# Ten low parts of weights formed by adding DMAs, and the first conv-out chunk split: a hybrid decoder layer on one core

## The chip, the cores and the metric

The kernel runs on 1 core of a Trainium2 chip. The metric is the device time of one execution in microseconds; the time before is the median of three runs.

## The reference, cut to what matters

One layer over 256 tokens of width 1024, float32 throughout. `n` is an RMS norm of the input. A combined projection of `n` gives a convolution branch, an attention branch and two gates; then come a cross attention, an MLP and a last norm.

```python
u = a * sigmoid(gate)                                    # conv branch, from n @ w_in
u = depthwise_conv(u, conv_w, 31 taps, causal) + conv_b
u = silu(layernorm(u, ln_g, ln_b))
y_conv = u @ w_conv_out
y_attn = top_k_attention(q, k, v, qi, ki, wi) @ w_attn_out   # 8 heads
h = x + (g_conv * y_conv + g_attn * y_attn) @ w_mix_out
h = h + cross_attention(rmsnorm(h), rmsnorm(mem))        # 4 heads, wx_q, wx_kv, wx_o
h = h + square(relu(rmsnorm(h) @ w_ff1)) @ w_ff2
return rmsnorm(h)
```

## The kernel before, in words

**Weights.** All weights come as a stream of chunks of 1 MB (128 partitions x 2048 float32), in the order of `STREAM` (line 34): conv 0 to 3, qi, ki, conv 4 to 7, gc (the gate of the conv branch), ga (the gate of the attention branch), v, q and k in turn, xk and xv (cross attention's keys and values), ao (attention out), co (conv out), mix, xq, xo, f1 and f2. Numbered from 0, chunk 8 is conv 5, chunk 35 is ao 0 and chunk 39 is co 0. `load` (line 154) issues a chunk's DMA on the SP queue into one of three `raw` buffers; chunks named in `EARLY` (line 58) get a buffer of their own out of a larger pool.

**Splitting.** A product in float32 is made of three products in float32r. Each chunk is split in two halves of 128x1024: ScalarE copies the half rounded to the high part `hi` (line 178), VectorE subtracts it from the raw half to give the low part `lo` (line 181). `high` does the first and queues the second as a job; `split_ahead` (line 213), called once in every tile, takes one low job and then one high job, so that up to five halves are ready ahead of TensorE. Six buffers of each part rotate. With the last low part of a chunk, the chunk's raw buffer is done with, and `load` is called for the next chunk. A tile of weights then is 8 steps of the contraction with three products each: high x high, high x low, low x high (`mm3`, line 247).

**Two whole chunks.** Chunks in `WHOLE` (line 59), conv 0 and co 0, are not split; their products run in float32 with the activations as they are (`form_b_whole`, line 302, for co 0). Its 16 products stand as 32 records in the trace.

**Forms.** `form_b` (line 274) does a chunk in two tiles of 24 products, each into one bank of PSUM out of `ps_mm`, which has two banks (tag "mm", line 141); after a tile its bank is evicted by ScalarE or VectorE (`after`). `form_b_late` (line 285) does both tiles but for the last steps of the contraction, then the last steps of both, then both evictions. `form_b_whole` took its two banks from `ps_acc`, which has four. `form_a` (line 569) does v and xv in quarters.

**Chains and fillers.** `tick` (line 218), called after each tile, lets every running chain (a generator: an attention head, the layer norm, the memory's norm) go one step on, and then fills VectorE with convolution taps out of `fill`, as long as the priced VectorE work stands behind the priced TensorE work (`Counted`, line 62). One tap is one `scalar_tensor_tensor` of VectorE; when a channel tile has its 31 taps, POOL adds it to `usum` (line 455). With the last of the eight tiles the chain `layer_norm` (line 595) is started: TensorE averages over channels (`ps_mub`), VectorE subtracts, ScalarE squares, TensorE sums (`ps_vr`), POOL takes the power (`rs_vr`), and, once all eight heads are done, ScalarE loads the Silu table, TensorE spreads the factors (`ps_rsb`), VectorE multiplies and ScalarE applies eight Silu (lines 620 to 625). Then `parts_of` (line 631) splits the result `u_p` in four steps of VectorE, one at a tick. co 0 as a whole chunk needs only the Silu's result, `acc`; co 1 to 3 need `u_p`.

**Around the change.** After the heads come four ao chunks (eight tiles, evicted by ScalarE to `ya`, line 318), then co; each co tile is gated by VectorE (`gated`, line 717) and split for mix.

Of the kernel before, what the change touches and what calls it, by code (L numbers as in the profile page):

```python
# [8 lines left out]
F32 = mybir.dt.float32  # L9
F32R = mybir.dt.float32r  # L10
BF16 = mybir.dt.bfloat16
AF = mybir.ActivationFunctionType
ALU = mybir.AluOpType
# [5 lines left out]
S = 256  # L19
KT = D // P  # L20
# [13 lines left out]
STREAM = (  # L34
    [("conv", i) for i in range(4)]
    + [("qi", i) for i in range(2)]
    + [("ki", 0)]
    + [("conv", i) for i in range(4, 8)]
    + [("gc", i) for i in range(4)]
    + [("ga", i) for i in range(4)]  # L40
    + [("v", i) for i in range(4)]
    + [(n, i) for i in range(4) for n in ("q", "k")]
# [12 lines left out]
NK = 72  # L55
N_CHUNK = KT * S
HALVES = 6
EARLY = (3, STREAM.index(("co", 0)))
WHOLE = (("conv", 0), ("co", 0))


class Counted:
# [49 lines left out]
def block_kernel(ctx, tc, x, xt, mem, memt, wst, wki, vecs, convw, gout, out):  # L112
    nc = tc.nc
    ctx.enter_context(tc.manual_schedule())
    pe = Counted(nc.tensor, pe_price)
    dve = Counted(nc.vector, dve_price)
    act = nc.scalar.activation
# [10 lines left out]
    def t8(name, dt=F32, shape=(P, KT, S)):  # L128
        return big.tile(list(shape), dt, tag="t8", bufs=12, name=name)
# [7 lines left out]
    def bank(tag, bufs, name):  # L137
        return psum.tile([P, 512], F32, tag=tag, bufs=bufs, name=name)
# [4 lines left out]
    def ps_acc(name):  # L143
        return bank("acc", 4, name)
# [5 lines left out]
    prepared, whole = {}, {}  # L150
# [3 lines left out]
    def load(parts=1):  # L154
        if nload[0] >= len(STREAM):
            return
        c = nload[0]
        nload[0] += 1
        key = STREAM[c]
        raw = t8(f"raw{c}", F32, (P, N_CHUNK)) if c in EARLY else raws.tile([P, N_CHUNK], F32, tag="raw", name=f"raw{c}")  # L160
        n = KT * NK if key[0] == "ki" else N_CHUNK
        src = wki if key[0] == "ki" else wst[INDEX[key]]
        for q in range(parts):
            ns = slice(q * n // parts, (q + 1) * n // parts)
            nc.sync.dma_start(raw[:, ns], src[:, ns])
        if key in WHOLE:
            whole[key] = raw.rearrange("p (k n) -> p k n", k=2 * KT)
            return
        parts = 1 if key[0] == "ki" else 2
        for q in range(parts):  # L170
            ns = slice(q * n // parts, (q + 1) * n // parts)
            high_jobs.append(lambda ns=ns, q=q, last=q == parts - 1: high(key, c, raw, ns, q, last))

    def high(key, c, raw, ns, q, last):
        n = ns.stop - ns.start
        hi = highs.tile([P, N_CHUNK // 2], F32R, tag="hi", name=f"hi{c}_{q}")[:, :n]
        lo = lows.tile([P, N_CHUNK // 2], F32R, tag="lo", name=f"lo{c}_{q}")[:, :n]
        act(hi, raw[:, ns], AF.Copy)  # L178

        def low():  # L180
            dve.tensor_tensor(out=lo, in0=raw[:, ns], in1=hi.bitcast(F32), op=ALU.subtract)
            prepared[(*key, q)] = (hi, lo)
            if last and c not in EARLY:
                load()

        low_jobs.append(low)

    def split_high():
        if high_jobs and nsplit[0] - nused[0] < HALVES - held[0]:
            nsplit[0] += 1  # L190
            high_jobs.pop(0)()

    def split_low():
        if low_jobs:
            low_jobs.pop(0)()
# [17 lines left out]
    def split_ahead():  # L213
        if not waiting[0]:
            split_low()
        split_high()

    def tick():
        for c in list(chains):
            if next(c, "end") == "end":  # L220
                chains.remove(c)
        while (len(fill) > 1 or (fill and (len(done) > 5 or nused[0] < 5))) and dve.total < pe.total - 1000:
            fill_one()
        dve.total = max(dve.total, pe.total - 2000)
# [10 lines left out]
    def finish(chain):  # L235
        while chain in chains:
            tick()

    def start(gen):
        chains.append(gen)  # L240
        return gen
# [28 lines left out]
    def is_wide(kind, ct):  # L270

        return kind == "f1" or (kind == "mix" and ct < 6)

    def form_b(kind, i, x2, after, ps_of=ps_mm):

        for ct in range(2):
            w = weights(kind, i, ct, KT)
            split_ahead()
            ps = ps_of(f"ps_{kind}{i}{ct}")
            wide = is_wide(kind, 2 * i + ct)  # L280
            tile_b(ps, w, x2, wide=wide)
            after(2 * i + ct, ps if wide else ps[:, :S])
            tick()

    def form_b_late(kind, i, x2, after, cuts=(KT - 1,), ps_of=None):
# [12 lines left out]
            after(2 * i + ct, banks[ct] if is_wide(kind, 2 * i + ct) else banks[ct][:, :S])  # L298
            tick()
        held[0] = 1  # L300

    def form_b_whole(kind, i, x, after, cuts):

        w = whole[(kind, i)]
        banks = [ps_acc(f"ps_{kind}{i}{ct}")[:, :S] for ct in range(2)]
        for lo, hi in zip((0, *cuts), (*cuts, KT)):
            for ct in range(2):
                for kt in range(lo, hi):
                    pe.matmul(banks[ct], w[:, ct * KT + kt, :], x[:, kt, :], start=kt == 0, stop=kt == KT - 1)
            split_ahead()  # L310
            if hi == KT:
                load()
            tick()
        for ct in range(2):
            after(2 * i + ct, banks[ct])

    def copy_to(dst):
        return lambda ct, ps: act(dst[:, ct, :], ps, AF.Copy)
# [120 lines left out]
    acc = t8("acc")  # L439
    usum = cst.tile([P, S], F32, tag="sums", bufs=2, name="usum")  # L440

    def tap(t, s):
        def go():
            j = TAPS - 1 - s
            if s == 0:
                act(acc[:, t, :], u[:, t, :], AF.Identity, scale=cw[:, t, j : j + 1], bias=cvb[:, t : t + 1])
            else:
                dve.scalar_tensor_tensor(out=acc[:, t, s:], in0=u[:, t, : S - s], scalar=cw[:, t, j : j + 1],
                                         in1=acc[:, t, s:], op0=ALU.mult, op1=ALU.add)
            if s == TAPS - 1:  # L450
                done.append(t)
                if len(done) == KT:
                    start(layer_norm())
                if len(done) > 1:
                    nc.gpsimd.tensor_tensor(out=usum, in0=usum if len(done) > 2 else acc[:, done[0], :],
                                            in1=acc[:, t, :], op=ALU.add)
        return go

    def conv_tile(i, half):
        key = ("conv", i)  # L460
        w = weights("conv", i, half, KT) if key not in WHOLE else None
        split_ahead()
# [8 lines left out]
    def conv_in(i):  # L471
# [8 lines left out]
        fill.append([tap(i, s) for s in range(1, TAPS)])  # L480
        if ("conv", i) in WHOLE:
            load()
# [105 lines left out]
        form_a("v", hf, n2, v_rm, (1.0, 1.0))  # L588


    u2 = []

    normed = []

    def layer_norm():
        u2.append(parts_t8("u_p"))
        yield
        mub = ps_aux("ps_mub")[:, :S]
        pe.matmul(mub, onesd, usum, start=True, stop=True)
        mub = mub.unsqueeze(1).to_broadcast([P, 2, S])  # L600
        vs = w2("vs", F32, (P, 2, S))
        pairs = [slice(2 * c, 2 * c + 2) for c in range(4)]
        for c, cs in enumerate(pairs):
            dve.tensor_tensor(out=acc[:, cs, :], in0=acc[:, cs, :], in1=mub, op=ALU.subtract)
            sq = vs if c == 0 else w2(f"sq_vr{c}", F32, (P, 2, S))
            act(sq, acc[:, cs, :], AF.Square)
            if c > 1:
                dve.tensor_tensor(out=vs, in0=vs, in1=before, op=ALU.add)
            before = sq
        waiting[0] = True  # L610
        yield
        waiting[0] = False
        dve.tensor_tensor(out=vs, in0=vs, in1=before, op=ALU.add)
        dve.tensor_tensor(out=vs[:, 0, :], in0=vs[:, 0, :], in1=vs[:, 1, :], op=ALU.add)
        yield
        rs = rsqrt(vs[:, 0, :], "vr")
        yield
        while len(headed) < NH:
            yield
        act(table, table, AF.Silu)  # L620
        rsb = spread(rs, "rsb").unsqueeze(1).to_broadcast([P, 2, S])
        for c, cs in enumerate(pairs):
            dve.tensor_tensor(out=acc[:, cs, :], in0=acc[:, cs, :], in1=rsb, op=ALU.mult)
            for t in (2 * c, 2 * c + 1):
                act(acc[:, t, :], acc[:, t, :], AF.Silu, scale=lng[:, t : t + 1], bias=lnb[:, t : t + 1])
        normed.append(True)
        for c in range(4):
            yield
            parts_of(2 * c)
# [52 lines left out]
    for i in range(4):  # L682
        q, k = qk(f"q{i}"), qk(f"k{i}")
# [20 lines left out]
        form_b("ao", i, o2, copy_to(ya))  # L704
    while fill:
        fill_one()
    while not normed:
        tick()


    h_t = t8("h_t")
# [18 lines left out]

    gate_branch(0)
    for i in range(4):
        if i == 0:
            form_b_whole("co", i, acc, gated, (2, 4, 6))
        else:
            form_b("co", i, u2[0], gated)
    low_due.pop()()


# [277 lines left out]
    for c in range(14):  # L1017
# [4 lines left out]
        for k in range(2):  # L1022
            w = weights("f2", c, k, 1)
# [102 lines left out]
```

## Time and profile before

| | before |
|---|---|
| median of 3 runs | 516.89 us (516.72 to 516.94) |
| the profiled execution | 516.86 us |
| its span | 515.1 us |
| granted TensorE clock, mean | 0.998 |
| busy: TensorE matmul / weight load | 504.3 / 463.1 us |
| busy: VectorE / ScalarE / POOL | 419.4 / 286.9 / 19.2 us |
| moved by DMA | 92.75 MB |

Lines of the profile read so: the engine, the operation, what it writes and reads by the program's names, shapes, then a count, busy time and mean. In a chain or timeline the first number is the start within the span and the second how long it took, both in us. In the list of waits the numbers behind the colon are us in total, times, longest. PE is TensorE, PEld its weight loads, DVE VectorE, ACT ScalarE, POOL GpSimd, SP SyncE; a small q behind it is the engine's queue. L77 is a helper that records most VectorE and TensorE operations, so groups are told apart by their tiles.

### The profile page before, as it was taken

What the parts mean: (1) busy time and instruction counts of PE and PEld (TensorE: products, weight loads), DVE (VectorE), ACT (ScalarE), POOL (GpSimd) and SP (SyncE); (2) the same over time, 40 slices, a digit from 0 to 9 for tenths busy, and PEclk for the clock granted to TensorE, in tenths of its full rate; (3) what the DMA queues carried; (4) which work ended last, traced back from release to release, by engine and by line L of the source; (5) the groups of instructions that cost most, each with busy time, mean ns of one, the idle gap of its engine ahead of it and who ended that gap; (6) DMA issues with size and microseconds to landing.
All of it is one profiled execution on the core that took longest, in us unless ns stands there. A gap on an engine that the chain in (4) does not pass through costs nothing.

```text
span 515.1 us, 8515 instructions
## 1 busy us (share of the span) xinstructions
PE 504.3 (98%) x3354; PEld 463.1 (90%) x3354; DVE 419.4 (81%) x796; ACT 286.9 (56%) x489; POOL 19.2 (4%) x30
## 2 busy tenths in 40 slices
PE   7999999999999999999999999999999999999995
PEld 5999999999899999999999998988888888888884
DVE  4998999999988999999898976696766566666565
ACT  5666655546446666656655657565654454554442
POOL 2000000001001000021000000000000000000000
PEclk9999999999999999999999999999999999999999
DMA  8856435464552343454744541446445554445402
GB/s 317 359 187 236 155 122 205 174 225 183 194 216 102 144 164 118 155 224 161 275 143 155 207 184 44 181 165 242 164 169 220 221 207 163 164 174 219 181 1 81
DMA packets 14311, 92.75 MB, mean 180 GB/s; under 512 B 1584, under 2 KB 2480, under 8 KB 3776
## 3 DMA queue, kind: packets, MB, share of 16 engines
q1 hardware_dynamic: 13952, 91.85, 48.3%
q8 instruction: 26, 0.43, 0.3%
q10 hardware_dynamic: 288, 0.33, 0.2%
q14 instruction: 13, 0.11, 0.1%
q0 software_dynamic: 32, 0.04, 0.0%
HBM read 91.16 MB, written 1.05 MB: 179 GB/s over the span
## 4 chain that ended last, share of the span: by engine, by line
PE 95%; issue 1%; ACT 1%; DVE 1%; DMA 1%; POOL 0%; POOLq 0%; DVEq 0%; ACTq 0%
PE ps_f L77 17%; PE ps_ff L77 16%; PE ps_conv L77 9%; PE ps_co L77 5%; PE ps_ao L77 4%; PE ps_ga L77 4%; PE ps_gc L77 4%; PE ps_k L77 4%; PE ps_q L77 4%; PE ps_mix L77 4%; PE ps_v L77 4%; PE ps_xo L77 3%; PE ps_xq L77 2%; PE ps_qi L77 2%; PE ps_xk L77 2%; PE ps_xv L77 2%
## 5 line engine op out<-in xcount | busy, mean ns | idle before, releaser
L77 DVE TENSOR_TENSOR lo<-raw,hi 128x1024 fp32r<-128x1024 f32 x161 | 195.7, 1225 | 3.3 <-ACT hi L178 1.6
L178 ACT ACTIVATE hi<-raw 128x1024 fp32r<-128x1024 f32 x161 | 166.4, 1047 | 2.5 <-PE ps_v L77 2.5
L77 DVE SCALAR_TENSOR_TENSOR acc<-u,cw,acc 128x255 f32<-128x255 f32 (+27 forms) x240 | 100.6, 475 | 0.6
L77 PE MATMUL ps_f<-ff_p,hi 128*128 128x512 f32 x256 | 89.8, 396 | 0.0
L77 PE MATMUL ps_ff<-hi,fs 128*128 128x512 f32 (+1 forms) x256 | 80.8, 387 | 0.0
L77 PE MATMUL ps_f<-ff_p,lo 128*128 128x256 f32 x256 | 66.2, 279 | 0.0
L77 PEld LDWEIGHTS ps_ff<-hi,fs 128*128 128x128 f32 x256 | 47.9, 188 | 9.2
L77 PEld LDWEIGHTS ps_f<-ff_p,hi 128*128 128x128 f32 x256 | 46.8, 188 | 9.2
L77 DVE TENSOR_TENSOR ft<-ps_f,ft 128x256 f32<-128x256 f32 x32 | 13.6, 423 | 46.4 <-ACT ft L957 46.4
L77 PEld LDWEIGHTS ps_f<-ff_p,lo 128*128 128x128 f32 x256 | 48.2, 188 | 2.6
L957 ACT ACTIVATE ft<-ps_f 128x256 f32<-128x256 f32 x32 | 12.2, 380 | 66.9 <-PE ps_f L77 66.9
L77 PE MATMUL ps_ff<-lo,fs 128*128 128x512 f32 (+1 forms) x128 | 49.4, 386 | 0.0
L77 PE MATMUL ps_conv<-n_p,hi 128*128 128x256 f32 x224 | 41.0, 285 | 0.0
L77 PEld LDWEIGHTS ps_conv<-n_p,hi 128*128 128x128 f32 x224 | 34.9, 192 | 0.8 <-issue 0.7
L77 PE MATMUL ps_conv<-n_p,lo 128*128 128x256 f32 x112 | 31.7, 283 | 0.0
L77 PEld LDWEIGHTS ps_ff<-lo,fs 128*128 128x128 f32 x128 | 24.1, 188 | 4.9
L77 PE MATMUL ps_q<-n_p,hi 128*128 128x256 f32 x128 | 24.4, 291 | 0.0
L77 PE MATMUL ps_ao<-o_p,hi 128*128 128x256 f32 x128 | 23.5, 285 | 0.0
L77 PE MATMUL ps_k<-n_p,hi 128*128 128x256 f32 x128 | 23.4, 284 | 0.0
L77 PE MATMUL ps_gc<-n_p,hi 128*128 128x256 f32 x128 | 23.1, 283 | 0.0
L77 PE MATMUL ps_ga<-n_p,hi 128*128 128x256 f32 x128 | 23.1, 283 | 0.0
L77 PE MATMUL ps_mix<-mix_p,hi 128*128 128x512 f32 (+1 forms) x80 | 22.1, 350 | 0.0
(229 smaller groups left out, 1003.3 us busy)
## 6 DMA issues: line engine op xcount, KB each, us to landing
raw<-in_wst_dram SPq DMA_DIRECT2D x80, 1024.0 KB, 4.8
raw<-in_wst_dram SPq DMA_DIRECT2D x4, 512.0 KB, 7.7
x_rm<-in_x_dram SPq DMA_DIRECT2D x2, 512.0 KB, 3.9
mem_rm<-in_mem_dram SPq DMA_DIRECT2D x1, 1024.0 KB, 9.0
mem_t<-in_memt_dram SPq DMA_DIRECT2D x1, 1024.0 KB, 11.0
h_t<-in_xt_dram SPq DMA_DIRECT2D x1, 1024.0 KB, 6.9
out_dram<-hg SPq DMA_DIRECT2D x4, 176.0 KB, 2.2
g_out<-in_gout_dram SPq DMA_DIRECT2D x1, 512.0 KB, 7.0
```

What stands on the lines that cost most here:

```text
L77: return fn(*args, **kwargs)
L178: act(hi, raw[:, ns], AF.Copy)
L957: act(t, ps[:, S:], AF.Copy)
```

## The change: ten DMAs that add, and one chunk split

For the second half of chunks 8, 11, 14, and so on to 35, ScalarE writes the negated high part into the low part's buffer right behind the high part, and the low job issues a DMA on POOL's queue that adds the raw half to it. The other low parts stay on VectorE. co 0 is no longer whole: it is split as every chunk is, read through one of the three raw buffers, and done in `form_b_late` (its cut is before the last of the eight steps) with the split activations. `form_b_whole` goes away. Ahead of co the program waits for the whole layer norm chain, parts and all, where it waited only for the Silu.

```diff
-EARLY = (3, STREAM.index(("co", 0)))
-WHOLE = (("conv", 0), ("co", 0))
+EARLY = (3,)
+WHOLE = (("conv", 0),)
...
+    def low_by_dma(key, c, q):
+
+        return q == 1 and c % 3 == 2 and 8 <= c < STREAM.index(("ao", 1))
+
     def high(key, c, raw, ns, q, last):
...
         act(hi, raw[:, ns], AF.Copy)
+        by_dma = low_by_dma(key, c, q)
+        if by_dma:
+            act(lo, hi.bitcast(F32), AF.Copy, scale=-1.0)
 
         def low():
-            dve.tensor_tensor(out=lo, in0=raw[:, ns], in1=hi.bitcast(F32), op=ALU.subtract)
+            if by_dma:
+                nc.gpsimd.dma_start(lo.bitcast(F32), raw[:, ns], accum_op=ALU.add)
+            else:
+                dve.tensor_tensor(out=lo, in0=raw[:, ns], in1=hi.bitcast(F32), op=ALU.subtract)
             prepared[(*key, q)] = (hi, lo)
             if last and c not in EARLY:
                 load()
...
-    def form_b_whole(kind, i, x, after, cuts):
...
                 if len(done) == KT:
-                    start(layer_norm())
+                    norms.append(start(layer_norm()))
...
-    while not normed:
-        tick()
+    finish(norms[0])
...
     for i in range(4):
-        if i == 0:
-            form_b_whole("co", i, acc, gated, (2, 4, 6))
-        else:
-            form_b("co", i, u2[0], gated)
+        (form_b_late if i == 0 else form_b)("co", i, u2[0], gated)
```

The low job priced itself to `Counted` as VectorE work; the DMA does not, so the fillers take that room and the taps, and with them the layer norm, come earlier in the built order.

More of the change, by code (lines that the diff above doesn't have):

```diff
@@ L300, in form_b_late @@
         held[0] = 1
-    def form_b_whole(kind, i, x, after, cuts):
[L304 to L312, printed above, removed]
-            tick()
-        for ct in range(2):
-            after(2 * i + ct, banks[ct])
     def copy_to(dst):
@@ L588, in block_kernel @@
         form_a("v", hf, n2, v_rm, (1.0, 1.0))
-    u2 = []
-    normed = []
+    u2, norms = [], []
     def layer_norm():
@@ L625, in layer_norm @@
                 act(acc[:, t, :], acc[:, t, :], AF.Silu, scale=lng[:, t : t + 1], bias=lnb[:, t : t + 1])
-        normed.append(True)
         for c in range(4):
@@ L706, in block_kernel @@
         fill_one()
-    while not normed:
-        tick()
+    finish(norms[0])
     h_t = t8("h_t")
```

## The prediction

> **What bounds the kernel now.** I read the page first: the span, the busy sums and the shares of the chain that ended last. The profiled execution took 516.86 us around its span of 515.1 us; the median shown is 516.89, so the two are one number here, and the sum below is made against 516.86.
>
> ```profile
> span 515.1 us, 8515 instructions
> ...
> PE 504.3 (98%) x3354; PEld 463.1 (90%) x3354; DVE 419.4 (81%) x796; ACT 286.9 (56%) x489; POOL 19.2 (4%) x30
> ...
> PE 95%; issue 1%; ACT 1%; DVE 1%; DMA 1%; POOL 0%; POOLq 0%; DVEq 0%; ACTq 0%
> ...
> L77 DVE TENSOR_TENSOR lo<-raw,hi 128x1024 fp32r<-128x1024 f32 x161 | 195.7, 1225 | 3.3 <-ACT hi L178 1.6
> L178 ACT ACTIVATE hi<-raw 128x1024 fp32r<-128x1024 f32 x161 | 166.4, 1047 | 2.5 <-PE ps_v L77 2.5
> ```
>
> The reader is to see that TensorE makes 95% of the chain. VectorE's 161 subtractions, which the change thins out, cost 1.225 us each but stand on no link of it. The second view is the list of waits of TensorE itself:
>
> ```profile
> PE ps_warm L350 <- DVE zero_r L335: 1.9, 1, 1.9
> PE pt_n L77 <- DVE ms_n L77: 1.3, 1, 1.3
> PE ps_xo L77 <- ACT xptr L853: 0.8, 1, 0.8
> PE pt_n L77 <- DVE x_rm L77: 0.4, 1, 0.4
> ```
>
> Three of these are the start, the third is in the cross attention near 314 us. So in the first half TensorE never waits for VectorE: **12 us less VectorE work is worth nothing by itself**. It can only pay through the products that TensorE is then given. The chain in order of time shows those:
>
> ```profile
> 75.73 23.04 PE ps_gc L77 x192
> ...
> 121.81 21.79 PE ps_v L77 x96
> ...
> 219.13 0.67 PE ps_o L77 x6
> 219.80 5.49 PE ps_xv L77 x24
> 225.29 11.51 PE ps_ao L77 x96
> 236.81 0.43 PE ps_mub L77 x2
> ...
> 242.99 0.34 PE ps_vr L77 x4
> ...
> 246.30 0.22 PE ps_rsb L77 x2
> 246.52 2.87 PE ps_ao L77 x24
> 249.39 24.18 PE ps_co L77 x176
> ```
>
> **The change part by part.** *The first conv-out chunk.* A tile of split weights is 24 products; 192 of them take 23.04 us, so 0.120 us each and 2.88 us a tile. The conv-out stage holds 176 records in 24.18 us: 144 split products (six tiles, 17.28 us) and 32 records of the whole float32 chunk, which leaves 6.90 us. Split, that chunk is 48 products, 5.76 us. **Gain 1.14 us.** It adds two halves on ScalarE (2 x 1.05 us) and two on VectorE (2 x 1.225 us), both hidden behind attention-out products as the other chunks' halves are.
>
> *The layer norm moves.* In the built order of the changed program the product of the mean (ps_mub) no longer stands after four attention-out tiles but right after the last head (ps_o), ahead of the last two quarters of xv; ps_vr follows them, then one attention-out tile, then ps_rsb, then the other seven. So the parts of u are done many tiles before conv-out needs them, which answers the question whether splitting makes conv-out wait. But the norm's work on ScalarE moves too, and that part was last seen here:
>
> ```profile
> 246.34 0.38 ACT L318 ACTIVATE ya<-ps_ao 128x256 f32<-128x256 f32 x1 [1.74 <-PE ps_ao L77]
> 246.73 1.28 ACT L620 ACT_TABLE_LOAD   x1
> 248.02 0.20 ACT L620 ACTIVATE table<-table 128x1 f32<-128x1 f32 x1
> 248.13 4.03 ACT L625 ACTIVATE acc<-acc,vec 128x256 f32<-128x256 f32 x8
> 252.07 1.04 ACT L178 ACTIVATE hi<-raw 128x1024 fp32r<-128x1024 f32 x1
> 253.02 0.36 ACT L318 ACTIVATE ya<-ps_ao 128x256 f32<-128x256 f32 x1
> ```
>
> From ps_rsb at 246.30 until the next eviction is over at 253.38 ScalarE needs 7.08 us: table load, eight Silu, a high part, the eviction. Before, this was the last attention-out tile; conv-out went on into other PSUM banks (ps_acc, four) and nobody waited. After, six more attention-out tiles follow, and their pool (ps_mm) has two banks. Counted from ps_rsb: 0.22 for it, 2.87 for the second tile, 2.88 for the third, so the fourth tile could start at 5.97 but needs the bank of the second, which is free at 7.08 plus some 0.04 for the signal. **Loss 1.15 us**, a new wait. Queued behind the Silu on ScalarE are the high part and that eviction; behind TensorE's wait stands the whole rest of its stream. After it, the third tile's eviction comes a high part later (1.0 + 0.4 us) while the fourth tile takes 2.88, so it does not repeat.
>
> *The variance.* ps_vr must wait until the squares are summed. Before, the norm's VectorE chain ran from 237.28 to 242.41:
>
> ```profile
> 237.28 1.88 DVE L77 TENSOR_TENSOR acc<-acc,ps_mub 128x512 f32<-128x512 f32 x3 [0.23 <-PE ps_mub L77]
> ...
> 241.99 0.42 DVE L77 TENSOR_TENSOR vs<-vs 128x256 f32<-128x256 f32 x1
> ...
> 258.09 0.42 DVE L77 TENSOR_TENSOR gc_t<-ps_co,gc_t 128x256 f32<-128x256 f32 x1
> ```
>
> ```profile
> 219.84 0.38 ACT L244 ACTIVATE o_p<-ps_o 128x256 fp32r<-128x256 f32 x1 [1.97 <-PE ps_o L77]
> ...
> 231.09 0.38 ACT L318 ACTIVATE ya<-ps_ao 128x256 f32<-128x256 f32 x1 [1.55 <-PE ps_ao L77]
> ```
>
> That is 5.13 us. After, it starts behind the last head's split: ScalarE to 220.22, VectorE about 0.42 more, 220.66, so the sums are ready at 225.8. TensorE comes to ps_vr at 219.80 + 0.43 + 5.49 = 225.72. **Loss 0.1 us** (0 to 0.3).
>
> *The late form of the first chunk.* It ends with three products of one bank and three of the other, and the next tile wants the first bank. The bank is full 3 x 0.12 = 0.36 us before the form's end; evictions start some 0.04 us after a tile's end (231.09 against 225.29 + 2 x 2.88 = 231.05); VectorE's gating product takes 0.42, the signal back 0.04. **Loss 0.14 us** (0 to 0.3). Before, this chunk had banks of its own.
>
> *The ten low parts.* Removed: 10 x 1.225 = 12.25 us of VectorE, hidden before and hidden gone. Added: ten negated copies on ScalarE, taken as the high part's 1.05 us each. In the gate stages ScalarE sits idle 1.46 us a tile, ahead of the eviction, which covers them; in the head stage, where less is idle, an eviction slips by some 0.1 us with a whole tile to spare. Added on POOL's queue: ten DMAs of 512 KB from SBUF to SBUF that read, add and write. They wait in order there, behind score selections, sums and the negated copies; what is queued behind them on POOL (the norm's sums and its power) has microseconds of room.
>
> ```profile
> 84.41 0.48 ACT L567 ACTIVATE gc_t<-ps_gc,vec 128x256 f32<-128x256 f32 x1 [1.46 <-PE ps_gc L77]
> 84.78 1.05 ACT L178 ACTIVATE hi<-raw 128x1024 fp32r<-128x1024 f32 x1
> ...
> 99.18 1.05 ACT L178 ACTIVATE hi<-raw 128x1024 fp32r<-128x1024 f32 x1
> ...
> 119.34 1.05 ACT L178 ACTIVATE hi<-raw 128x1024 fp32r<-128x1024 f32 x1
> ```
>
> ```profile
> raw<-in_wst_dram SPq DMA_DIRECT2D x80, 1024.0 KB, 4.8
> ...
> x_rm<-in_x_dram SPq DMA_DIRECT2D x2, 512.0 KB, 3.9
> ...
> mem_t<-in_memt_dram SPq DMA_DIRECT2D x1, 1024.0 KB, 11.0
> ```
>
> ```profile
> 1.24 0.75 POOL L325 DMA_DIRECT2D vec<-in_vecs_dram  x1 [0.79 <-POOLq L1117]
> ...
> 92.01 0.33 SPq L165 DMA_DIRECT2D raw<-in_wst_dram  x1
> ```
>
> No adding DMA is in the trace, so its time D, from the end of the negated copy, is bounded: at least 3.9 us (512 KB, plain), at most 11.0 (1 MB among other transfers). I take 6: a load of 1 MB is as many bytes as both operands here (4.8), plus POOL's issue (0.75), plus sharing. What it may take: chunk 14's second half has its high part at 84.78, so its negated copy ends near 86.9, and its tile, the eighth of gc, starts at 75.73 + 7 x 2.88 = 95.9: room 9.0 us. Chunk 20 is the tightest: 119.34 + 2.1 = 121.4 against the fourth quarter of ps_v at 121.81 + 3 x 2.72 = 130.0, room 8.5. The other eight, counted alike, have 9.0 to 12. The raw buffer comes free when the DMA lands: chunk 17's load, issued at 92.01, would start at 86.9 + 6 = 92.9, land 4.8 later at 97.7, and ScalarE wants it at 99.18. So at 6 us **the cost is nothing**, by cover that ends at D = 8.5.
>
> The Trainium skill, "DMA: Bandwidth & Descriptors", section "Anatomy of one DMA — SWDGE (gpsimd) path", gives such a DMA about 2.0 us plus its bytes at 436 GB/s, an estimate of 3.2 us for 512 KB; "Collectives: The Full Stack", section on the bandwidth ceiling and the fold count, says an adding transfer is slower because it needs two source reads, which makes the estimate 4.4 us. By either the sum would be the same, and no run yet shows an adding DMA.
>
> *Sum:* -1.14 + 1.15 + 0.1 + 0.14 = +0.25 us; **516.86 + 0.25 = 517.1 us**. The new stalls give back what the shorter products save.
>
> **The rivals.** (1) *The Silu wait does not come*, because the eviction gets out earlier than the rows say or the bank is free for another reason: then -1.14 + 0 to 0.25, 515.7 to 516.0 us. Against it: the built order puts the eight Silu ahead of that eviction, and the pool has two banks. (2) *The adding DMA is late* (the other side, slower): it decides from D = 8.5 us. At D = 10 the rooms of chunks 8 to 20 (10.0, 9.5, 9.0, 9.0, 8.5) are overrun by 0, 0.5, 1.0, 1.0 and 1.5, in all 4.0 us: 521.1 us. At 11.0, the bound, about 11 us: 528. For it: it shares 16 engines that the loads keep about half busy, and reads twice what it writes. Against it: 6 us leaves 2.5. (3) *The relief does not do what it says*: VectorE lags, the norm's parts come where they came before, and the late form waits for them. The last pair was done near 258.2, as gating follows it at 258.09; the form would want it some 2.2 us after 249.39, so it waits about 6.5 us and the time is near 522. Against it: the built order has the norm six tiles earlier.
>
> **How the numbers follow.** About 0.2% (1.03 us) is what a measurement of this kernel can tell from no change: faster is under 515.86, slower over 517.92. The forecast (516.4 to 517.9): 0.64. Rival 1: 0.10, most of it under 515.86. Rival 2: 0.22. Rival 3: 0.04. So faster 0.08, same 0.64, slower 0.28. The range takes in the forecast, rival 1 down to 515.7, and rival 2 up to D = 10: 515.7 to 521.2.
>
> **What would show it.** Conv-out should take 23.0 to 23.2 us in the chain with no record of acc and raw. A wait of TensorE's attention-out on ScalarE's ya near 235 us, of 1.0 to 1.3 us, shows the new stall; if it is missing, the time is a microsecond lower. The issue list shows D as the time to landing of the ten lo transfers; any wait of TensorE on a DMA shows rival 2. A TensorE wait on u_p shows rival 3. If waits of TensorE on VectorE appear in the head stage, I have misread the cover.

## The result, and the profile after

The changed kernel takes 518.53 us (median of six runs, 518.50 to 519.23), the kernel before 516.84 beside it: a ratio of 1.0036, 95% interval 1.0023 to 1.0049. It is slower by 1.69 us, where 0.25 was forecast. The profiled execution is the longest of the six, 519.23 us: a load at the kernel's start landed 12.4 us after its issue, long before the first adding DMA at 49.8 us, and moved everything behind it by 0.73 us. This stands in front of all that the change touches and is left out of the sums below: what is compared are lengths of stages.

The page of the changed kernel first: span, busy sums, the shares of the chain that ended last, then one of the costliest groups and the issues of the adding DMAs.

```profile
span 517.4 us, 8588 instructions
...
PE 504.4 (97%) x3370; PEld 463.0 (89%) x3370; DVE 410.4 (79%) x788; ACT 299.1 (58%) x501; POOL 24.5 (5%) x40
...
PE 86%; DVE 6%; DMA 2%; ACT 2%; issue 2%; SPq 0%; POOLq 0%; POOL 0%; DVEq 0%; ACTq 0%
...
L77 DVE TENSOR_TENSOR lo<-raw,hi 128x1024 fp32r<-128x1024 f32 x153 | 185.1, 1220 | 7.8 <-ACT hi L182 6.2
...
lo<-raw POOLq DMA_DIRECT2D x10, 512.0 KB, 5.8
```

VectorE has 9 us less to do and ScalarE 12 us more; TensorE does as much as before, but its share of the chain fell from 95% to 86%. An adding DMA took 5.8 us (median) from the start of POOL's issue to landing. The forecast's D = 6 was counted from the end of the negated copy; counted so in the trace, the ten took 4.8 to 8.9 us, median 6.7. Nine were issued 0.3 us after the copy's end. The tenth, chunk 29's, was issued 3.9 us after it (copy done at 177.31), because POOL's queue stood behind a sum of taps that waited for VectorE:

```profile
180.45 0.83 POOL L450 TENSOR_TENSOR usum<-usum,acc 128x256 f32<-128x256 f32 x1 [23.49 <-DVE acc L77]
181.23 0.85 POOL L189 DMA_DIRECT2D lo<-raw  x1
```

The list of TensorE's waits shows who took the place in the chain (after, one column: us in total, times, longest):

```profile
PE ps_ao L77 <- ACT ya L313: 1.2, 1, 1.2
...
PE ps_vr L77 <- DVE vs L77: 0.2, 1, 0.2
PE ps_co L77 <- DVE gc_t L77: 0.2, 1, 0.2
```

A fourth stands in the list of the weight loads, and none of the two lists has a wait on a lo transfer or on u_p:

```profile
PEld ps_gc L77 <- DVE u L77: 0.3, 1, 0.3
```

The chain in order of time gives their full price (after; start, length, what). A piece that runs on without a pause is counted from the end of the record before it:

```profile
34.90 5.16 PE ps_qi L77 x43
...
79.06 0.35 DVE u L77
...
79.45 20.42 PE ps_gc L77 x168
99.87 1.20 PE ps_ga L77 x10
...
220.24 0.68 PE ps_o L77 x6
...
226.97 0.58 PE ps_vr L77 x4
227.54 2.97 PE ps_ao L77 x24
230.52 0.23 PE ps_rsb L77 x2
...
237.34 0.27 ACT ya L313
...
237.66 14.66 PE ps_ao L77 x120
252.32 5.42 PE ps_co L77 x45
...
257.76 0.43 DVE gc_t L77
...
258.24 17.54 PE ps_co L77 x144
```

Each wait has two parts: the gap, and a longer run of products behind it. At 0.120 us a product, 120 products of attention-out are 14.40 us, but 14.66 stand there; 144 of conv-out are 17.28 against 17.54; 168 of gc 20.16 against 20.42. **Each restart costs 0.26 us beyond its gap** (where it comes from, the last section tells). The four, gap and restart:

- *ya*: two tiles behind ps_rsb end at 230.75 + 5.76 = 236.51; the fourth tile starts at 237.66. 1.15 + 0.26 = 1.41 us.
- *gating*: 48 products from 252.32 end at 258.08; the next tile starts at 258.24. 0.16 + 0.26 = 0.42.
- *sums*: ps_mub (0.43) and xv (5.49) behind 220.92 end at 226.84; ps_vr starts at 226.97 and takes 0.58 for 0.34. 0.13 + 0.24 = 0.37.
- *gc*: the ga stage starts 1.10 us later than before (98.77), of which 0.73 stands already in front of qi (34.90 for 34.17 in before's chain). 0.37 us. It does not come of the late load: the kernel with the late form in four banks, below, has qi at 34.20 in its profile and ga at 99.16, 0.36 us late.

With the gain of 1.14 that is -1.14 + 1.41 + 0.42 + 0.37 + 0.37 = +1.43 us of the measured 1.69. Of the 0.26 left, some 0.1 stands behind TensorE's last record, and the rest is open.

### The profile page after: what moved, and what is told of

The parts are those of the page before. It is cut to its first block, busy times and chain, and to the rows that moved or that the text cites. A ratio compares the mean times of both kernels' runs of the same rounds, so it can differ in the third digit from the quotient of the medians.

```text
span 517.4 us, 8588 instructions
## 1 busy us (share of the span) xinstructions
PE 504.4 (97%) x3370; PEld 463.0 (89%) x3370; DVE 410.4 (79%) x788; ACT 299.1 (58%) x501; POOL 24.5 (5%) x40
## 4 chain that ended last, share of the span: by engine, by line
PE 86%; DVE 6%; DMA 2%; ACT 2%; issue 2%; SPq 0%; POOLq 0%; POOL 0%; DVEq 0%; ACTq 0%
PE ps_f L77 17%; PE ps_ff L77 16%; PE ps_ga L77 4%; PE ps_k L77 4%; PE ps_q L77 4%; PE ps_co L77 4%; PE ps_mix L77 4%; PE ps_v L77 4%; PE ps_gc L77 4%; PE ps_conv L77 4%; PE ps_ao L77 3%; PE ps_xo L77 3%; DMA raw<-in_wst_dram 2%; PE ps_xq L77 2%; PE ps_qi L77 2%; PE ps_xk L77 2%
## 5 line engine op out<-in xcount | busy, mean ns | idle before, releaser
L77 DVE TENSOR_TENSOR lo<-raw,hi 128x1024 fp32r<-128x1024 f32 x153 | 185.1, 1220 | 7.8 <-ACT hi L182 6.2
L182 ACT ACTIVATE hi<-raw 128x1024 fp32r<-128x1024 f32 x163 | 168.4, 1047 | 4.6 <-DMA raw<-in_wst_dram 3.1
L77 DVE SCALAR_TENSOR_TENSOR acc<-u,cw,acc 128x235 f32<-128x235 f32 (+22 forms) x240 | 99.6, 470 | 0.5
L77 PE MATMUL ps_co<-u_p,hi 128*128 128x256 f32 x128 | 23.2, 284 | 0.2 <-DVE gc_t L77 0.2
## 6 DMA issues: line engine op xcount, KB each, us to landing
mem_t<-in_memt_dram SPq DMA_DIRECT2D x1, 1024.0 KB, 10.1
```

What stands on the lines that cost most here:

```text
L77: return fn(*args, **kwargs)
```

## The experiments

The theory: the change gains 1.14 us in conv-out and loses it to four waits of TensorE, each with its own cause; none of the transfers is late. Its rivals: the waits hide one another, so that taking one away moves it elsewhere; and the adding DMAs themselves, by their transfers or the negated copies, cost the time. Each edit is made to the changed kernel, but for one that says so. A ratio's interval is some 0.1% (0.5 us) wide to each side, so a difference of 0.4 us between two medians is not clear of it; that a wait of this size is gone is shown by its stage in the trace.

**Attention-out in four banks.** The order of every engine stays.

```diff
-        form_b("ao", i, o2, copy_to(ya))
+        form_b("ao", i, o2, copy_to(ya), ps_acc)
```

> The changed kernel with one edit: the attention-out tiles take their PSUM banks from the pool of four (ps_acc) instead of the pool of two (ps_mm); the order of every engine is the same. Theory: the fourth attention-out tile waits only for a bank that ScalarE frees behind the table load and the eight Silu. Between the record starts of the changed kernel that wait cost 1.44 us, so it should go: 518.5 - 1.44 = 517.1 us, and the list of waits of TensorE has no ya. Rival: the wait only stands in front of something else that ScalarE delivers late behind the Silu (a high part of the weights, the split u_p); then a wait of about the same length appears two to six tiles later and the time stays at 518.2 to 518.5.

Measured: 517.10 us (516.93 to 517.88, 11 runs), ratio to before 1.0005 (0.9997 to 1.0014): 1.43 us less than the changed kernel. In its chain the seven tiles behind ps_rsb now run through:

```profile
230.78 20.15 PE ps_ao L77 x168
```

168 x 0.120 = 20.16: no gap, no restart. ScalarE still evicts late; nobody waits for it. The wait was a matter of banks, all of it, and nothing else took its place: the rival fell.

**The late form of conv-out in four banks.**

```diff
-        (form_b_late if i == 0 else form_b)("co", i, u2[0], gated)
+        (form_b_late if i == 0 else form_b)("co", i, u2[0], gated, ps_of=ps_acc if i == 0 else ps_mm)
```

> The changed kernel with one edit: the late form of the first conv-out chunk takes its two banks from the pool of four, so that the next chunk's first tile finds a free bank. Theory: conv-out loses its wait on VectorE's gating, 0.42 us between record starts: 518.5 - 0.42 = 518.1 us, conv-out 23.04 us (192 x 0.120). Rival: the gating itself is late (two tiles end together and VectorE does four products for them), so the wait moves to the third tile and the time stays at 518.5.

Measured: 518.13 us (517.81 to 518.76, 8 runs), ratio 1.0025 (1.0014 to 1.0035): 0.40 less. Its chain has the stage in one piece, so the wait did not move to the third tile and the rival fell:

```profile
251.62 23.04 PE ps_co L77 x192
```

**The sum one tile later.**

```diff
+        yield
         rs = rsqrt(vs[:, 0, :], "vr")
```

> The changed kernel with one edit: the layer norm takes one step more ahead of the summing product ps_vr, so that it stands one attention-out tile later (2.88 us), and ps_rsb with the Silu one tile later too. Theory: the wait of ps_vr for the summed squares goes, 0.37 us between record starts, and the wait on ya stays as it is, one tile later: 518.5 - 0.37 = 518.1 us. Rival: the one tile's shift changes which high parts stand between the Silu and the evictions, so that the wait on ya becomes longer by up to a high part (1.05 us), 518.1 to 519.2 us.

Measured: 518.15 us (518.01 to 518.91, 8 runs), ratio 1.0025 (1.0015 to 1.0035): 0.38 less. The wait on vs is gone (ps_vr takes 0.34 us again), the one on ya is 1.2 us as it was, a tile later. The rival fell.

**Nine DMAs: chunk 8 back on VectorE.**

```diff
-        return q == 1 and c % 3 == 2 and 8 <= c < STREAM.index(("ao", 1))
+        return q == 1 and c % 3 == 2 and 11 <= c < STREAM.index(("ao", 1))
```

> The changed kernel with nine adding DMAs instead of ten: the low part of chunk 8 stays on VectorE. Theory: without it three convolution taps are drawn into its place, and these stand behind a wait for ScalarE, so that VectorE comes to the last convolution products 1.7 us later and the gc stage waits 0.38 us for a bank; with chunk 8 back on VectorE gc takes 23.04 us and the time is 518.5 - 0.4 = 518.1 us. Rival: the wait in gc comes of the other lows, of the negated copies on ScalarE or of the raw loads; then it stays and so does 518.5 us.

Measured: 518.87 us (518.32 to 519.38, 5 runs), ratio 1.0037 (1.0025 to 1.0050). **The time was missed, the cause was not.** The gc stage is whole again; its row in the chain, and then a row of the list of waits:

```profile
75.82 23.04 PE ps_gc L77 x192
```

```profile
PE ps_vr L77 <- DVE vs L77: 0.4, 1, 0.4
```

What gc gained came back at ps_vr, whose record starts 6.53 us after that of ps_mub, for 6.23: VectorE's chain of the norm is 0.3 us later. By its stages this kernel should be 0.1 us below the changed one; that its median of five isn't stays open.

Why gc waits is seen on VectorE's timeline near 52 us. The changed kernel, and below it the one with nine DMAs (start, length, what, in brackets the idle time before):

```profile
51.59 0.85 DVE L77 SCALAR_TENSOR_TENSOR acc<-u,cw,acc 128x244 f32<-128x244 f32 x2
53.14 0.48 DVE L77 SCALAR_TENSOR_TENSOR mem_p<-mem_t,vec,mem_p 128x256 fp32r<-128x256 f32 x1 [0.70 <-ACT mem_p L375]
...
53.63 3.88 DVE L77 SCALAR_TENSOR_TENSOR acc<-u,cw,acc 128x243 f32<-128x243 f32 x10
...
78.98 0.42 DVE L77 TENSOR_TENSOR u<-ps_conv,sg 128x256 f32<-128x256 f32 x1
```

```profile
50.96 0.85 DVE L77 SCALAR_TENSOR_TENSOR acc<-u,cw,acc 128x244 f32<-128x244 f32 x2
51.73 1.22 DVE L77 TENSOR_TENSOR lo<-raw,hi 128x1024 fp32r<-128x1024 f32 x1
...
53.34 2.74 DVE L77 SCALAR_TENSOR_TENSOR acc<-u,cw,acc 128x243 f32<-128x243 f32 x7
...
77.57 0.42 DVE L77 TENSOR_TENSOR u<-ps_conv,sg 128x256 f32<-128x256 f32 x1
```

In place of the subtraction (1.22 us) VectorE idles 0.70 us for ScalarE's mem_p, and then does three taps more (3.88 - 2.74 = 1.14 us). The account that draws taps in knows priced work, not idle time, so it paid 1.14 us for a room of 0.52. VectorE never makes that up before the last convolution products, whose bank gc wants: u comes at 78.98, against 77.57. Of these 1.41 us some 0.6 is the start's delay (the two taps ahead, 51.59 and 50.96), and 0.8 the taps.

**Chunk 8 by DMA, but without the taps.** That still leaves the transfer itself as a cause; this one keeps it and takes the taps away.

```diff
                 nc.gpsimd.dma_start(lo.bitcast(F32), raw[:, ns], accum_op=ALU.add)
+                if c == 8:
+                    dve.total += dve.price(n, (), {})
```

> The changed kernel with one edit: the adding DMA of chunk 8 books the subtraction's price on VectorE's account, so that no convolution taps are drawn into the room it leaves; the DMA itself stays. Against the kernel with nine DMAs, VectorE has one subtraction less and its other instructions in the same order. Theory: the wait in gc comes of the three taps that took the subtraction's place, not of the DMA: gc 23.04 us, ps_vr waits 0.3 us longer as with nine DMAs, 518.4 us or so. Rival: the wait comes of chunk 8's transfer (a raw buffer that comes free late, a negated copy in ScalarE's way); then gc stays at 23.4 us and the time at 518.5 to 518.9 us.

Measured: 518.44 us (518.23 to 519.34, 7 runs), ratio 1.0029 (1.0018 to 1.0040), as forecast, though the time alone does not part this from the rival's 518.5. The chain does:

```profile
76.14 23.04 PE ps_gc L77 x192
```

The ten DMAs and their negated copies are in place, and ps_vr waits 0.4 us as with nine. The taps did it, not the transfer.

**The DMAs alone**: the kernel before with `low_by_dma`, the negated copy and the adding DMA, and nothing else.

```diff
...
+        by_dma = low_by_dma(key, c, q)
+        if by_dma:
+            act(lo, hi.bitcast(F32), AF.Copy, scale=-1.0)
...
+            if by_dma:
+                nc.gpsimd.dma_start(lo.bitcast(F32), raw[:, ns], accum_op=ALU.add)
...
```

> The kernel before with the ten adding DMAs alone; the first conv-out chunk stays whole and in float32. Theory: the DMAs by themselves are hidden, but the taps that fill VectorE's room bring the layer norm forward, and with it come the waits on ya (1.44 us), on the sums (0.37) and in gc (0.38): 516.94 + 2.2 = 519.1 us; conv-out stays at 24.18 us. Rival (less work on VectorE is worth nothing and costs nothing): 516.9 us.

Measured: 519.43 us (519.25 to 520.38, 5 runs), ratio 1.0052 (1.0038 to 1.0066). Conv-out takes 24.18 us as before, and the waits on ya, on the sums and in gc are there (1.2 and 0.2 us in the list of products, 0.3 in that of the weight loads). The theory held, with 0.3 us more than it summed up; that the rival's 516.9 failed shows that less work on VectorE can cost time.

**The split alone**: none of the DMAs.

```diff
-        return q == 1 and c % 3 == 2 and 8 <= c < STREAM.index(("ao", 1))
+        return False
```

> The changed kernel with none of the ten adding DMAs, all low parts on VectorE: the first conv-out chunk split, done in the late form, after the whole layer norm. Theory: the norm stays where it was (ps_mub after four attention-out tiles), so there is no wait on ya and none of the sums, but the late form comes before the parts of u are ready and waits for them: 516.94 - 1.14 + 0.4 for the gating + 4 to 6.5 for u_p, 520.2 to 522.7 us. So the ten DMAs are what makes the split possible. Rival: the parts come pair by pair as the products want them, and the wait is under 1 us: 516.2 to 517.2 us, and the DMAs were not needed.

Measured: 519.38 us (519.08 to 519.87, 5 runs), ratio 1.0045 (1.0032 to 1.0058): between the theory's bounds and the rival's. The chain of this kernel around conv-out:

```profile
249.16 1.14 DVE lo L77
250.30 0.35 DVE u_p L77
...
250.67 1.04 DVE u_p L77 x2
...
253.86 0.70 DVE u_p L77
...
254.61 3.38 PE ps_co L77 x26
```

The parts come pair after pair behind one subtraction of weights, and the form eats them as they come. The wait is 519.38 - (516.94 - 1.14 + 0.42) = 3.2 us, where the theory had 4 to 6.5. In the kernel before, a subtraction of weights stood in front of every pair, so that the last one was done at 258.17; these are its rows:

```profile
255.89 1.22 DVE L77 TENSOR_TENSOR lo<-raw,hi 128x1024 fp32r<-128x1024 f32 x1
...
257.48 0.69 DVE L77 TENSOR_TENSOR u_p<-acc,u_p 128x512 fp32r<-128x512 f32 x1
```

Here the last pair is done at 254.56, 3.6 us earlier. With the norm where it stands without the DMAs, the split costs more than it gains: alone each half of the change costs 2.4 to 2.5 us, together they cost 1.7.

**All ten booked on VectorE's account**: the same line as for chunk 8, without its condition.

> The changed kernel with one edit: each of the ten adding DMAs books the subtraction's price on VectorE's account, so that no taps are drawn forward; TensorE's order is that of the kernel without any of the DMAs. VectorE has ten subtractions (12.2 us) less to do. Theory: what the ten DMAs change is the order alone, by the taps and the norm that they draw forward; with the norm where it was, the time is that of the kernel with no DMAs, 519.4 us, with the wait on u_p (3.1 us in all) in front of and in conv-out and none on ya or in gc. Rival: a VectorE with 12 us less work is ahead by itself, the parts of u come earlier and the wait on u_p shrinks by 1 us or more: under 518.4 us.

Measured: 520.24 us (519.61 to 520.91, 5 runs), ratio 1.0066 (1.0052 to 1.0080). Conv-out takes 25.2 us as in the split alone, and the wait on u_p is the same 1.5 us, two times, in both lists. 12 us less work on VectorE brought nothing by itself; what the DMAs buy comes through the order of the taps. Whether VectorE could keep that earlier order with the ten subtractions still on it, no run shows. The profiled executions (519.61 and 519.37) differ by 0.24 us, and the chain has it in attention-out, 11.75 us for 11.51: a weight load waits 0.2 us for the last of the ten transfers, which was issued 4.9 us after its negated copy, behind a sum on POOL's queue that waited for VectorE. The rest of the 0.9 us between the medians is open; the three longer executions show a granted clock of 0.993 to 0.994, the two shorter ones 0.996, as the profiled one of the split alone does.

**Nineteen DMAs.**

```diff
-        return q == 1 and c % 3 == 2 and 8 <= c < STREAM.index(("ao", 1))
+        return q == 1 and c % 3 != 1 and 8 <= c < STREAM.index(("ao", 1))
```

> The changed kernel with nineteen adding DMAs instead of ten (the second half of two chunks in three, from chunk 8 on). In the built order the norm comes earlier again: ps_mub and ps_vr stand among the heads and ps_rsb ahead of the last two quarters of xv, whose banks are not those of attention-out. Theory (the transfers stay under their cover, only the moved norm has a price): the waits on ya (1.44 us) and on the sums (0.37) go, the gating's 0.42 and gc's 0.4 (up to 0.8 with two subtractions fewer ahead of it) stay: 518.5 - 1.8 = 516.7 us, 516.5 to 517.2. Rival (the adding DMA is late when the queue is denser): the time to landing goes from 5.8 to 8.5 us or more, TensorE waits for lo transfers, 518 to 525 us.

Measured: 523.49 us (521.96 to 524.21, 4 runs), ratio 1.0123 (1.0108 to 1.0138). The theory fell. The rival's waits and its time came, its cause only in part: the median time to landing rose to 6.8 us, not to 8.5. The list of TensorE's waits, and the time to landing (least, median, most) of the transfers of ten and of nineteen:

```profile
PE ps_ga L77 <- DMA lo<-raw: 1.7, 1, 1.7
PE ps_gc L77 <- DMA lo<-raw: 1.5, 1, 1.5
PE ps_k L77 <- DMA lo<-raw: 1.3, 1, 1.3
...
PE ps_gc L77 <- DVE u L77: 0.8, 1, 0.8
...
PE ps_q L77 <- DMA lo<-raw: 0.3, 1, 0.3
```

```profile
DMA to landing us min/median/max: 4.5/5.8/7.4
```

```profile
DMA to landing us min/median/max: 4.5/6.8/10.1
```

Five waits of 5.6 us in all and five restarts (1.3), with the gating's 0.42 and the gain of 1.14, make 516.88 + 6.2 = 523.1. The waits on ya and on the sums are gone, as the norm stands earlier.

The four transfers that TensorE waits for landed 10.5 to 11.3 us after the end of their negated copy. Those for ga and k were long under way, 10.0 and 8.8 us from the issue. The one for gc took 6.3, as among the ten, but had waited 4.7 us on POOL's queue (copy done at 76.11), behind a score selection that waited for VectorE; the one for q took 7.8 behind 3.5 in the queue:

```profile
80.25 0.28 POOL L503 TENSOR_SCALAR_AFFINE_SELECT score<-score 128x128 f32<-128x128 f32 x1 [9.27 <-DVE score L77]
80.81 0.88 POOL L189 DMA_DIRECT2D lo<-raw  x1 [0.28 <-issue]
```

Late transfers also hold up the loads, since a raw buffer comes free when its adding DMA has landed: ScalarE's idle time that a raw load ended ahead of the high parts is 21.2 us here and 3.1 in the changed kernel.

**The four remedies together**: four banks for both, the sum a tile later, chunk 8 on VectorE.

> The changed kernel with the four edits together: attention-out and the late form of conv-out in the pool of four banks, ps_vr one tile later, chunk 8's low part back on VectorE. Theory: the change is a gain of 1.14 us (the first conv-out chunk in split products) under four waits; the waits were 1.44 (ya), 0.37 (ps_vr), 0.42 (gating) and 0.38 us (the bank in gc), so without them the time is 516.94 - 1.14 = 515.8 us, faster than before; gc 23.04 and conv-out 23.04 us, and no wait of TensorE on ya, vs, gc_t or u. Chunk 8 back on VectorE alone made ps_vr 0.30 us later; the tile in front of ps_vr covers that. Rival: the waits overlap with something that every edit shifts (loads, high parts), so that they do not add up; then 516.5 to 517.

Measured: 516.15 us (515.75 to 516.85, 11 runs), ratio 0.9981 (0.9972 to 0.9990): **faster than before**, by 0.8 us of the 1.14. None of the four waits is in its list, and its chain goes from the last head to mix on TensorE alone, of which these are the rows of attention-out and conv-out:

```profile
226.56 2.87 PE ps_ao L77 x24
229.43 0.34 PE ps_vr L77 x4
...
232.96 17.27 PE ps_ao L77 x144
250.23 23.04 PE ps_co L77 x192
```

Counted from the start of qi (34.94 here, 34.17 before), conv-out ends 1.07 us earlier than before, so nearly all of the gain is there. What the 0.35 us above the 515.8 expected are, in front of qi or behind conv-out, is open, like the 0.26 of the changed kernel. Nothing was run with the four remedies one short, so which of them could be left out is not shown.

## Why the prediction was right and wrong

- **Right: the gain.** 1.14 us, to the hundredth (24.18 to 23.04 in the kernels whose gating wait is gone).
- **Right: the three waits, in place, cause and gap.** 1.15, 0.14 and 0.1 us were forecast; the gaps are 1.15, 0.16 and 0.13. Taking away their cause one at a time took each of them away, in the trace.
- **Wrong: their price.** The three terms "Loss 1.15", "Loss 0.14" and "Loss 0.1" count the gap alone. Each has a restart of 0.24 to 0.26 us behind it, 0.76 in all; the medians of the experiments fell by 1.43, 0.40 and 0.38, the last two no more than their intervals. This is the larger part of the miss, and puts the time past the bound of 517.92.
- **Wrong: "Removed: 10 x 1.225 = 12.25 us of VectorE, hidden before and hidden gone."** It looked at what is removed, and not at the taps that come into its place. For chunk 8 they stand behind an idle stretch, so VectorE came later, not earlier, and gc waited 0.37 us. The section on the change said already that the fillers take that room; the prediction followed them to the norm and not to the next bank.
- **Right in the outcome: the transfers.** None of the ten was waited for. But D as the prediction defined it, from the end of the negated copy, was 4.8 to 8.9 us (median 6.7) for 6, and what stands ahead on POOL's queue, named without a price, cost one of them 3.9 us: that one passed the 8.5 at which the tightest cover was said to end, on a chunk that was given more room (9 to 12). With nineteen, transfers of up to 10.4 us went by unnoticed and those from 10.5 on were waited for, so the runs do not test the 8.5 itself. The two estimates from the Trainium skill, 3.2 us ("DMA: Bandwidth & Descriptors", section "Anatomy of one DMA — SWDGE (gpsimd) path") and 4.4 with two source reads ("Collectives: The Full Stack", section on the bandwidth ceiling and the fold count), are both under the least of the ten, 4.5 us from issue to landing.
- **Luck: the range.** The forecast proper, 516.4 to 517.9, missed 518.53. The range up to 521.2 holds it, but that part was there for late DMAs, and none was late; most of the 0.28 given to a time over 517.92 was for them.
- **The rivals.** The Silu wait came (rival 1 false). No DMA was late (rival 2 false at ten; at nineteen TensorE waits, in part through POOL's queue). The norm did move (rival 3 false); where it does not, in the split alone, the wait is 3.2 us and not 6.5, since the prediction took the last pair's time from the kernel before, where subtractions of weights stand between the pairs; without them it is done 3.6 us earlier.

The mechanism was right but for the fourth wait. Of the 1.44 us missed, 0.76 are the restarts, 0.37 the wait in gc and 0.05 the gaps' excess over the forecast; the other 0.26 are not accounted for, but for some 0.1 behind TensorE's last record.

## What to carry to other kernels

A wait of TensorE within a run of products costs its gap and a restart, 0.24 to 0.26 us here; where small gaps are weighed against a small gain, count the restarts. When work is taken off an engine whose schedule fills up by priced work, ask what is drawn into the room, behind what it will stand, and who waits for the next thing on that engine. And before a chain is moved forward, look at the banks of the tiles it will stand among: here four banks in place of two, out of a pool that the program had already, took 1.43 us off the changed kernel.

## What the runs showed of the hardware

The restart is the point not expected. TensorE's timeline around the wait in gc (changed kernel):

```profile
79.05 0.28 PE L77 MATMUL ps_gc<-n_p,lo 128*128 128x256 f32 x1
79.45 0.51 PE L77 MATMUL ps_gc<-n_p,hi 128*128 128x256 f32 x2
79.79 0.29 PE L77 MATMUL ps_gc<-n_p,lo 128*128 128x256 f32 x1
```

A product's record is 0.28 us long, but in a steady run the next starts 0.12 after it. A wait exposes the difference, 0.16, since its gap is counted from a modelled end; and the first pair takes 0.34 us to the next start where a steady one takes 0.24, another 0.10. Together 0.26. By starts alone, which need no modelled end, the next product comes 0.40 us after the last (79.05 to 79.45) for 0.12, which with the 0.10 makes 0.38, the price of this wait in the sum above (0.37). The Trainium skill, "TensorE: Matmul & The Clock Gate", section "Single matmul latency", gives (398 + N) / 2.4 ns for a single bf16 product at full clock, an estimate of 0.27 us for N = 256. The record's 0.28 lies next to it, but these products are not bf16 and the ends of their records are modelled, so no run here measures that latency; the 0.10 is beyond what it says.

The adding DMA of 512 KB within SBUF, beside the loads of weights, took 4.5 to 7.4 us from issue to landing in the changed kernel (ten in 177 us), up to 8.4 in the other kernels with nine or ten, and 4.5 to 10.1 with nineteen. POOL's issue, 0.87 us, is counted in. What waits on POOL's queue in front of the issue comes on top: up to 3.9 us in the changed kernel, 4.9 with all ten booked.
